# A low-rank gate as one contraction of 80 rows, and a rotary key whose weight parts share one tile

## The chip, the cores and the metric

The kernel runs on one core of a Trainium2 chip. The metric is the device time of one execution in microseconds (us). Before the change the median of three runs is 1384.74 us (1384.51 to 1385.14).

## The reference, cut to what matters

The model is a decoder trunk of two layers over 512 tokens of width 1024, in float32. Layer 0 mixes a Mamba-2 part (SSD) and gated linear attention (GLA), layer 1 is multi-head latent attention (MLA); each is followed by a SwiGLU FFN of hidden width 2816. Two small products matter here. In layer 0 the GLA forget gate comes from 16 columns of the input projection (`gk_low`) through a 16 x 512 matrix:

```python
gk = jax.nn.log_sigmoid((gk_low @ gk_w2 + gk_b).astype(jnp.float32)) / GLA_GATE_NORM
gcum = jnp.cumsum(gk.reshape(bsz, nc, Q, H, DK), axis=2)
...
q_dec = q * jnp.exp(gcum).astype(dtype)
k_inv = k * jnp.exp(-gcum).astype(dtype)
```

In layer 1 the last 32 columns of `h @ w_dqkv` are the rotary key that all 16 heads share:

```python
cq, ckv, k_rope = jnp.split(h @ w_dqkv, [MLA_Q_RANK, MLA_Q_RANK + MLA_KV_RANK], axis=-1)
...
k_rope = apply_rope(rms_norm(k_rope, k_rope_norm), cos, sin)
```

## The kernel before, in words

Activations lie transposed, features on the partitions and the 512 tokens along the free dimension, in eight tiles of 128 x 512. A dense product is computed on TensorE in the type fp32r: both factors are split into a rounded part and the remainder (`hi`, `lo`), and `mm3` (L140) issues three matmuls per tile of the contraction, hi by hi, hi by lo and lo by hi, all into one PSUM bank. `dense` (L145) runs `mm3` over the eight tiles of the contraction, so a block of 128 output features costs 24 matmuls of 512 columns.

`weight` (L124) brings the weights of a block: one DMA on SP's queue into a `wraw` tile (2 buffers), a cast on ScalarE into `whi` (L135, 3 buffers), a subtraction on VectorE into `wlo` (L136, 3 buffers).

The order on each engine is set by a planner when the program is built. It walks the program with timing estimates of its own and gives each engine, among the instructions whose operands and buffers are free, the one that stands earliest in the program. `weight` moves its three instructions 90 places forward in that order (`AHEAD`, L25). On the chip each engine then runs its list strictly in that order and waits on semaphores.

Three places matter for the change.

- L257 to L261: a 48-column projection gives 16 step sizes (rows 0 to 15) and `gk_low` (rows 32 to 47); VectorE scales it into `dg`. Four transposes (L269) read rows 0 to 15, and the step sizes go on from there, beside the convolutions (L313) of the SSD part, whose first products are the matmuls of L340.
- L470 to L489: behind the SSD part the pool `gla` opens in the memory that the SSD pool used. `w2`, the 16 x 512 gate matrix, is loaded on ScalarE's queue. For each of four heads one matmul in plain fp32 (L481: 16 rows, 128 x 512 out) writes the PSUM bank `st`, of which there is one; ScalarE takes the absolute value (L482), VectorE the minimum (L483). Then come one exponential (L484), one logarithm (L485), a subtraction (L486) and four scans (L488). `inner(0)` multiplies queries and keys by exponentials of the scan (L513, L529), and the matmuls of L548 to L550 read these. `out_round(1)`, half of the first two thirds of an output projection, is traced inside `inner(0)` and supplies other matmuls meanwhile.
- L689 to L693: at the start of MLA, behind FFN 0, a 32-column `dense` gives the rotary key (24 matmuls with 32 output rows), copied into `krr`. Five 128-column blocks of the same input follow (L700 to L702, `w_dqkv`), and then the transposes of `krr` (L739). The 32-column weights come through `weight`, so 90 places early.

A ring of two 128 x 512 tiles in the pool `res` with the tag `sq` holds squares for the norms: those of `Norm` (L196), `ysq` of the SSD part (L460) and `osq` of GLA (L586).

Of the kernel before, what the change touches and what calls it, by code (L numbers as in the profile page):

```python
# [8 lines left out]
F32 = mybir.dt.float32  # L9
F32R = mybir.dt.float32r  # L10
I32 = mybir.dt.int32
AF = mybir.ActivationFunctionType
ALU = mybir.AluOpType
# [4 lines left out]
P = 128  # L18
T = 512
D = 1024  # L20
KD = 8
# [24 lines left out]
def kernel(ctx: ExitStack, tc: tile.TileContext, A, yT, stop=99):  # L46
    nc = tc.nc
    V, S, G, E = nc.vector, nc.scalar, nc.gpsimd, nc.tensor

    const = ctx.enter_context(tc.tile_pool(name="const", bufs=1))  # L50
    res = ctx.enter_context(tc.tile_pool(name="res", bufs=1))
    wp = ctx.enter_context(tc.tile_pool(name="wp", bufs=3))
# [5 lines left out]
    def nm(s):  # L58
        cnt[0] += 1
        return f"{s}_{cnt[0]}"  # L60

    def acc():
        return pacc.tile([P, T], F32, tag="acc", name=nm("acc"))
# [11 lines left out]
    def aux(tag="st"):  # L75
        while isinstance(phase["tags"][tag], str):
            tag = phase["tags"][tag]
        return phase["p"].tile([P, T], F32, tag=tag, name=nm(tag), bufs=phase["tags"][tag])
# [13 lines left out]
    def col(name, i=0, lo=0, hi=P):  # L92
        j = PV[name] + i
        return pv[lo:hi, j:j + 1]
# [29 lines left out]
    def weight(src, kc, m):  # L124

        with tc.high_priority(offset=AHEAD):
            return weight_now(src, kc, m)

    def weight_now(src, kc, m):
        raw = wp.tile([P, KD * P], F32, tag="wraw", name=nm("wraw"), bufs=2)  # L130
        r = raw[:, :kc * m]
        nc.sync.dma_start(r.rearrange("p (k m) -> p k m", k=kc), src)
        hi = wp.tile([P, KD * P], F32R, tag="whi", name=nm("whi"))
        lo = wp.tile([P, KD * P], F32R, tag="wlo", name=nm("wlo"))
        S.copy(hi[:, :kc * m], r)  # L135
        V.tensor_tensor(lo[:, :kc * m], r, hi.bitcast(F32)[:, :kc * m], ALU.subtract)  # L136
        return (hi[:, :kc * m].rearrange("p (k m) -> p k m", k=kc),
                lo[:, :kc * m].rearrange("p (k m) -> p k m", k=kc))

    def mm3(out, ah, al, bh, bl, first, last):  # L140
        E.matmul(out, ah, bh, start=first, stop=False)  # L141
        E.matmul(out, ah, bl, start=False, stop=False)  # L142
        E.matmul(out, al, bh, start=False, stop=last)  # L143

    def dense(ps, w, xs):  # L145

        n = len(xs)
        for k, (xh, xl) in enumerate(xs):
            mm3(ps, w[0][:, k, :], w[1][:, k, :], xh, xl, k == 0, k == n - 1)
# [82 lines left out]
    R = nrm.done()  # L232
    xp = nrm.parts
# [20 lines left out]
    with tc.tile_pool(name="gkp", bufs=1) as gkp:  # L254
        rtok = tok_scalar(R)

        w = weight(A["w_dtgk"], KD, 48)  # L257
        ps = aux("a1")
        dense(ps[:48], w, xp)
        dg = gkp.tile([48, T], F32, name="dg")  # L260
        V.tensor_tensor(dg, ps[:48], R[:48], ALU.mult)  # L261
        dtb = gkp.tile([P, 16], F32, name="dtb")
        nc.scalar.dma_start(dtb, A["dt_bias"].partition_broadcast(P))
        alog = gkp.tile([P, 16], F32, name="alog")
# [2 lines left out]
        ps = aux()  # L267
# [26 lines left out]
        ps = aux()  # L294
# [6 lines left out]
        ps = aux()  # L301
# [6 lines left out]
        with tc.tile_pool(name="ssd", bufs=2) as sp:  # L308
            cw = sp.tile([P, 60], F32, name="cw", bufs=1)
            j = PV["conv_w"]  # L310
# [136 lines left out]
            for f in range(8):  # L447
# [12 lines left out]
                sq = res.tile([P, T], F32, tag="sq", name=nm("ysq"), bufs=2)  # L460
# [9 lines left out]
        with tc.tile_pool(name="gla", bufs=2) as gp:  # L470
            rmask = gp.tile([P, T], F32, name="rmask", bufs=1)
            G.memset(rmask, 1.0)
            G.memset(rmask.rearrange("p (c j) -> p c j", c=8)[:, :, 0:1], 0.0)
            w2 = gp.tile([48, T], F32, name="w2", bufs=1)
            nc.scalar.dma_start(w2[32:48, :], A["gk_w2"])

            ga = gp.tile([P, 4, T], F32, name="ga", bufs=1)
            gm = gp.tile([P, 4, T], F32, name="gm", bufs=1)
            for h in range(4):
                ps = aux()  # L480
                E.matmul(ps, w2[32:48, h * P:(h + 1) * P], dg[32:48, :], start=True, stop=True)  # L481
                S.activation(ga[:, h, :], ps, AF.Abs, bias=col("gk_b", h))  # L482
                V.tensor_scalar(gm[:, h, :], ps, col("gk_b", h), 0.0, ALU.add, ALU.min)  # L483
            S.activation(ga, ga, AF.Exp, scale=-1.0)  # L484
# [180 lines left out]
    R = mla_norm.done()  # L665
    xp = mla_norm.parts
    with tc.tile_pool(name="mla", bufs=2) as mp, tc.tile_pool(name="mla1", bufs=1) as m1:
# [18 lines left out]
                        pattern=[[-1, P]], channel_multiplier=1)  # L686


        w = weight(A["w_kr"], KD, 32)  # L689
        ps = acc()  # L690
        dense(ps[:32], w, xp)
        krr = m1.tile([32, T], F32, name="krr")
        V.tensor_copy(krr, ps[:32])  # L693


        lora, cf = {}, {}
        for who, n0, n in (("q", 0, 3), ("kv", 3, 2)):
            lora[who], ssq = [], None
            for c in range(n):
                w = weight(A["w_dqkv"][n0 + c], KD, P)  # L700
                ps = acc()
# [7 lines left out]
                sq = res.tile([P, T], F32, tag="sq", name=nm("lsq"), bufs=2)  # L709
# [4 lines left out]
            ps = aux()  # L714
# [22 lines left out]
        ps = aux()  # L737
# [14 lines left out]
        ps = aux()  # L752
# [247 lines left out]
```

## Time and profile before

| | |
|---|---|
| median of three runs | 1384.74 us |
| the profiled execution | 1385.21 us |
| its span on the core | 1383.5 us |
| TensorE (PE) busy | 1357.4 us, 98% of the span |
| VectorE (DVE) busy | 782.3 us, 57% |
| ScalarE (ACT) busy | 558.9 us, 40% |
| GpSimd (POOL) busy | 8.0 us, 1% |

The profile is of one execution. An engine is busy while it has an instruction in flight; matmuls are pipelined, so a matmul's own duration (0.39 us for 512 columns in fp32r) is longer than the distance from one start to the next. The chain of waits follows the work that ended last backwards and gives each piece of it the time by which it moved the end. "Idle before" in brackets is how long an engine stood before an instruction, and whose end it waited for. PEld is the weight load of TensorE, ACTq and SPq are the queues from which ScalarE and SyncE issue DMAs.

### The profile page before, as it was taken

Reading aid. Unit: us, or ns where it says so; the run is one execution under the profiler, and the core shown is the slowest. Engines: PE = TensorE matmul, PEld = TensorE weight load, DVE = VectorE, ACT = ScalarE, POOL = GpSimd, SP = SyncE. Lnnn points to the kernel's source line nnn. Section 1 sums busy time; section 2 is a strip of 40 time slices with the busy share of each in tenths; the row PEclk is TensorE's granted clock in tenths of the full one; section 3 lists DMA queues with packets and bytes.
Section 4 is the critical chain, followed back from the end, with each engine's and each line's share of the span. In section 5 each row is a group of like instructions: output and inputs, shape, how many; then the busy total and the mean of one; then the engine's idle time right before and its main releaser. Section 6 shows DMA issues by size and latency. Waiting matters only on the chain.

```text
span 1383.5 us, 16956 instructions
## 1 busy us (share of the span) xinstructions
PE 1357.4 (98%) x6650; PEld 1094.1 (79%) x6650; DVE 782.3 (57%) x1375; ACT 558.9 (40%) x934; POOL 8.0 (1%) x38
## 2 busy tenths in 40 slices
PE   7999999999999999999999999999999999999998
PEld 5798888677788888888888787667588888888887
DVE  7877966767757444444333449876684444443221
ACT  5675623543334323323223238775653233232221
POOL 0000000000000000000000000000000000000000
PEclk9999999999999999999999999999999999999999
DMA  5343132212233233233333321111032333333331
GB/s 175 108 143 102 61 106 78 63 61 76 62 105 93 91 93 106 92 98 100 92 90 107 90 66 59 52 46 62 1 92 91 103 95 92 101 97 107 104 108 64
DMA packets 36719, 122.19 MB, mean 88 GB/s; under 512 B 4736, under 2 KB 5760, under 8 KB 36640
## 3 DMA queue, kind: packets, MB, share of 16 engines
q1 hardware_dynamic: 35600, 120.70, 28.4%
q8 instruction: 53, 0.87, 0.3%
q10 hardware_dynamic: 1040, 0.41, 0.1%
q14 instruction: 26, 0.21, 0.0%
HBM read 118.96 MB, written 2.13 MB: 88 GB/s over the span
## 4 chain that ended last, share of the span: by engine, by line
PE 91%; DVE 6%; ACT 1%; issue 1%; DMA 1%; SPq 0%; ACTq 0%; DVEq 0%
PE acc L142 27%; PE acc L141 27%; PE acc L143 27%; PE sco L853 2%; PE ptr L867 1%; PE po L876 1%; DVE wlo L136 1%; PE st L175 1%; PE a L409 1%; PE a L579 1%; ACT whi L135 1%; PE a L395 0%; DMA x<-in_xT_dram 0%; PE a L581 0%; PE a L413 0%
## 5 line engine op out<-in xcount | busy, mean ns | idle before, releaser
L135 ACT CAST whi<-wraw 128x1024 fp32r<-128x1024 f32 (+2 forms) x223 | 226.7, 1018 | 570.9 <-PE acc L142 510.1
L141 PE MATMUL acc<-xh,whi 128*128 128x512 f32 (+1 forms) x1152 | 452.5, 393 | 2.8 <-ACT qT L836 1.6
L143 PE MATMUL acc<-xh,wlo 128*128 128x512 f32 (+1 forms) x1152 | 452.0, 393 | 0.0
L142 PE MATMUL acc<-xl,whi 128*128 128x512 f32 (+1 forms) x1152 | 451.7, 392 | 0.0
L136 DVE TENSOR_TENSOR wlo<-wraw,whi 128x1024 fp32r<-128x1024 f32 (+2 forms) x223 | 263.0, 1180 | 177.4 <-ACT whi L135 177.0
L141 PEld LDWEIGHTS acc<-xh,whi 128*128 128x128 f32 (+1 forms) x1152 | 215.7, 187 | 49.3 <-ACT qT L836 1.8
L142 PEld LDWEIGHTS acc<-xl,whi 128*128 128x128 f32 (+1 forms) x1152 | 215.8, 187 | 47.3 <-issue 3.3
L143 PEld LDWEIGHTS acc<-xh,wlo 128*128 128x128 f32 (+1 forms) x1152 | 215.8, 187 | 45.0 <-issue 0.9
L141 PE MATMUL acc<-fhh,whi 128*128 128x512 f32 x288 | 112.0, 389 | 0.0
L142 PE MATMUL acc<-fhl,whi 128*128 128x512 f32 x288 | 112.0, 389 | 0.0
L143 PE MATMUL acc<-fhh,wlo 128*128 128x512 f32 x288 | 112.0, 389 | 0.0
L637 DVE TENSOR_TENSOR fu<-acc,R 128x512 f32<-128x512 f32 x44 | 30.4, 691 | 139.4 <-PE acc L143 139.4
L634 DVE TENSOR_TENSOR fg<-acc,R 128x512 f32<-128x512 f32 x44 | 30.4, 692 | 94.0 <-PE acc L143 90.1
L143 PEld LDWEIGHTS acc<-fhh,wlo 128*128 128x128 f32 x288 | 54.1, 188 | 11.2
L141 PEld LDWEIGHTS acc<-fhh,whi 128*128 128x128 f32 x288 | 54.1, 188 | 11.2
L142 PEld LDWEIGHTS acc<-fhl,whi 128*128 128x128 f32 x288 | 54.1, 188 | 11.2
L141 PE MATMUL acc<-mxh,whi 128*128 128x512 f32 x128 | 49.7, 391 | 1.3 <-ACT whi L135 1.3
L142 PE MATMUL acc<-mxl,whi 128*128 128x512 f32 x128 | 49.9, 391 | 0.0
L143 PE MATMUL acc<-mxh,wlo 128*128 128x512 f32 x128 | 49.8, 390 | 0.0
L853 PE MATMUL sco<-kT,qT 96*128 96x128 f32 (+3 forms) x128 | 42.8, 445 | 1.5 <-DVE mx L856 1.3
L858 ACT ACTIVATE sc<-sc,mx 128x128 f32<-128x128 f32 (+3 forms) x64 | 35.7, 561 | 7.3 <-DVE mx L856 7.0
L856 DVE CUSTOM_DVE_ANT_0 sc<-sco,am 128x128 f32<-128x128 f32 (+3 forms) x64 | 30.7, 487 | 13.6 <-PE sco L853 11.5
(290 smaller groups left out, 1546.8 us busy)
## 6 DMA issues: line engine op xcount, KB each, us to landing
wraw<-in_w_gate_dram SPq DMA_DIRECT2D x44, 512.0 KB, 3.6
wraw<-in_w_up_dram SPq DMA_DIRECT2D x44, 512.0 KB, 3.6
wraw<-in_w_down_dram SPq DMA_DIRECT2D x32, 512.0 KB, 3.6
wraw<-in_w_out_dram SPq DMA_DIRECT2D x16, 512.0 KB, 3.6
wraw<-in_w_xbc_dram SPq DMA_DIRECT2D x12, 512.0 KB, 3.7
wraw<-in_w_down_dram SPq DMA_DIRECT2D x16, 384.0 KB, 3.1
wraw<-in_w_z_dram SPq DMA_DIRECT2D x8, 512.0 KB, 3.7
wraw<-in_w_v_dram SPq DMA_DIRECT2D x8, 512.0 KB, 3.6
```

Of the source, the lines that this page charges most:

```text
L135: S.copy(hi[:, :kc * m], r)
L136: V.tensor_tensor(lo[:, :kc * m], r, hi.bitcast(F32)[:, :kc * m], ALU.subtract)
L141: E.matmul(out, ah, bh, start=first, stop=False)
L142: E.matmul(out, ah, bl, start=False, stop=False)
L143: E.matmul(out, al, bh, start=False, stop=last)
L175: E.matmul(pb[:, c * P:(c + 1) * P], sel[:, c, :], y, start=True, stop=True)
L409: E.matmul(pd[64 * h:64 * h + 64, c * P:(c + 1) * P], xdt[:, c, h, :], mt[:, h, c, :], start=True, stop=True)
L634: V.tensor_tensor(g, pg, R, ALU.mult)
L637: V.tensor_tensor(u, pu, R, ALU.mult)
L853: E.matmul(ps[:, :n], qts[j][:, b * P:(b + 1) * P], kts[j][:, :n], start=True, stop=True)
L856: V.tensor_tensor_reduce(sc[:, :n], ps[:, :n], am[:, T - n:], -scale, 3e38, ALU.add, ALU.min, mx[:, j:j + 1])
L858: S.activation(sc[:, :n], sc[:, :n], AF.Exp, bias=mx[:, j:j + 1], scale=-1.0, accum_out=sm[:, j:j + 1])
```

## The change

The gate's factors are split too, but the three products are laid one below the other in one contraction. `gx` holds `gk_low` rounded in rows 0 to 15 and 32 to 47 and its remainder in rows 64 to 79; `gw` holds the remainder of the gate matrix in rows 0 to 15 and the rounded matrix in rows 32 to 47 and 64 to 79. The other rows are zero. One fp32r matmul of 80 rows per head replaces the fp32 matmul of 16 rows. `dg`, `w2` and the scratch tile `wt` come from the ring `sq`; `gx` and `gw` take the places of `dg` and `w2`.

For the rotary key the rounded weights lie twice and the remainder once side by side in one tile, 96 columns per tile of the contraction. Two matmuls per tile (with the high and the low part of the input) replace three; the remainder's product comes out in PSUM rows 64 to 95 and is added to rows 0 to 31. The weights no longer go through `weight`: their load, two casts and one subtraction stand at their own place in the program.

```diff
-        dg = gkp.tile([48, T], F32, name="dg")
-        V.tensor_tensor(dg, ps[:48], R[:48], ALU.mult)
+        dg = res.tile([P, T], F32, tag="sq", name="dg", bufs=2)
+        V.tensor_tensor(dg[:48], ps[:48], R[:48], ALU.mult)
+        gx = gkp.tile([80, T], F32R, name="gx")
+        G.memset(gx.bitcast(I32), 0)
+        S.copy(gx[32:48, :], dg[32:48, :])
+        S.copy(gx[0:16, :], dg[32:48, :])
+        V.tensor_tensor(gx[64:80, :], dg[32:48, :], gx[32:48, :].bitcast(F32), ALU.subtract)
...
-            w2 = gp.tile([48, T], F32, name="w2", bufs=1)
-            nc.scalar.dma_start(w2[32:48, :], A["gk_w2"])
+            gw = gp.tile([80, T], F32R, name="gw", bufs=1)
+            G.memset(gw.bitcast(I32), 0)
+            w2 = res.tile([P, T], F32, tag="sq", name="w2", bufs=2)
+            wt = res.tile([P, T], F32R, tag="sq", name="wt", bufs=2)
+            for j in (0, 32, 64):
+                nc.scalar.dma_start(w2[j:j + 16, :], A["gk_w2"])
+            S.copy(wt[0:16, :], w2[0:16, :])
+            V.tensor_tensor(gw[0:16, :], w2[0:16, :], wt[0:16, :].bitcast(F32), ALU.subtract)
+            for j in (32, 64):
+                S.copy(gw[j:j + 16, :], w2[j:j + 16, :])
...
-                E.matmul(ps, w2[32:48, h * P:(h + 1) * P], dg[32:48, :], start=True, stop=True)
+                E.matmul(ps, gw[:, h * P:(h + 1) * P], gx, start=True, stop=True)
...
-        w = weight(A["w_kr"], KD, 32)
+        wkr = wp.tile([P, KD * P], F32, tag="wraw", name="wkr", bufs=2)
+        wkr = wkr[:, :KD * 32].rearrange("p (k m) -> p k m", k=KD)
+        nc.sync.dma_start(wkr, A["w_kr"])
+        w3 = wp.tile([P, KD * P], F32R, tag="whi", name="w3")
+        w3 = w3[:, :KD * 96].rearrange("p (k j m) -> p k j m", k=KD, j=3)
+        for j in range(2):
+            S.copy(w3[:, :, j, :], wkr)
+        V.tensor_tensor(w3[:, :, 2, :], wkr, w3[:, :, 0, :].bitcast(F32), ALU.subtract)
         ps = acc()
-        dense(ps[:32], w, xp)
+        for k, (xh, xl) in enumerate(xp):
+            wk = w3[:, k].rearrange("p j m -> p (j m)")
+            E.matmul(ps[:96], wk, xh, start=(k == 0), stop=False)
+            E.matmul(ps[:96], wk, xl, start=False, stop=(k == KD - 1))
         krr = m1.tile([32, T], F32, name="krr")
-        V.tensor_copy(krr, ps[:32])
+        S.copy(krr, ps[64:96])
+        V.tensor_tensor(krr, ps[:32], krr, ALU.add)
```

## Rows read from the trace of the kernel before

**Rows 1.** The page: busy time, share of the span, instructions of each engine.
```profile
PE 1357.4 (98%) x6650; PEld 1094.1 (79%) x6650; DVE 782.3 (57%) x1375; ACT 558.9 (40%) x934; POOL 8.0 (1%) x38
```

**Rows 2.** Waits of PE over the span: us in total, times, longest.
```profile
PE a L548 <- DVE ki L529: 1.6, 1, 1.6
...
PE acc L141 <- ACT whi L135: 1.3, 1, 1.3
```

**Rows 3.** Chain of waits around the first gate matmul: start, us, what.
```profile
238.49 1.05 PE st L481 x2
239.53 0.43 PE acc L142
239.97 0.23 PE acc L143
```

**Rows 4.** Timeline: first matmul of the rotary key, first behind its last; start, us, what.
```profile
786.64 0.39 PE L141 MATMUL acc<-xh,whi 128*32 128x512 f32 x1
...
792.62 0.39 PE L141 MATMUL acc<-xh,whi 128*128 128x512 f32 x1
```

**Rows 5.** Timeline from the gate matrix's load to where PE stands waiting.
```profile
235.54 0.34 ACTq L475 DMA_DIRECT2D w<-in_gk_w_dram  x1
235.65 0.53 POOL L472 MEMSET rmask<- 128x512 f32 x1 [82.98 <-DVE mxl L121]
236.03 1.06 ACT L135 CAST whi<-wraw 128x1024 fp32r<-128x1024 f32 x1 [1.75 <-PE acc L142]
...
239.57 0.69 ACT L482 ACTIVATE ga<-st,pv 128x512 f32<-128x512 f32 x1 [2.49 <-PE st L481]
...
240.29 0.75 DVE L483 TENSOR_SCALAR gm<-st,pv 128x512 f32<-128x512 f32 x1 [1.95 <-ACT ga L482]
...
241.50 1.12 PE L481 MATMUL st<-dg,w 16*128 16x512 f32 x2
...
248.83 0.69 ACT L482 ACTIVATE ga<-st,pv 128x512 f32<-128x512 f32 x1 [2.40 <-PE st L481]
...
263.96 0.69 DVE L529 TENSOR_TENSOR ki<-kr,e 128x512 f32<-128x512 f32 x1
...
264.70 0.27 PE L548 MATMUL a<-qd,ki 128*64 128x64 f32 x1 [1.63 <-DVE ki L529]
...
266.33 0.47 PE L141 MATMUL acc<-mxh,whi 128*128 128x512 f32 x1 [1.29 <-ACT whi L135]
```

**Rows 6.** Timeline: last reader of a tile of the ring sq, ScalarE behind it.
```profile
223.29 0.69 DVE L463 TENSOR_TENSOR ysq<-ysq,ysq 128x512 f32<-128x512 f32 x1 [0.70 <-ACT ysq L461]
...
226.60 0.47 ACT L443 ACTIVATE v<-acc,rtok 128x256 f32<-128x256 f32 x1 [2.98 <-PE acc L143]
```

**Rows 7.** Timeline: subtractions that free a raw weight tile, around the rotary key.
```profile
787.70 1.22 DVE L136 TENSOR_TENSOR wlo<-wraw,whi 128x1024 fp32r<-128x1024 f32 x1 [0.17 <-ACT whi L135]
...
793.79 1.22 DVE L136 TENSOR_TENSOR wlo<-wraw,whi 128x1024 fp32r<-128x1024 f32 x1
```

**Rows 8.** DMA issues by line: count, KB each, median us to landing.
```profile
wraw<-in_w_kr_dram SPq DMA_DIRECT2D x1, 128.0 KB, 2.1
```

**Rows 9.** The tile krr: ns min/median/max, first and last start in us.
```profile
L739 PE MATMUL sco<-ident,krr x4: 221/222/243, 827.9 to 828.1; 32*128 32x32 f32 x4
```

**Rows 10.** Timeline around the scaled projection dg and the first SSD products.
```profile
29.93 0.68 DVE L261 TENSOR_TENSOR dg<-a,R 48x512 f32<-48x512 f32 x1 [0.68 <-ACT R L177]
...
39.22 0.68 DVE L330 SCALAR_TENSOR_TENSOR cT<-cvt,cva 128x512 f32<-128x512 f32 x1
...
39.95 0.19 PEld L340 LDWEIGHTS a<-cT,bT 128*128 128x128 f32 x1
```

**Rows 11.** A stretch at the start: us, busy us (count) by engine, PEclk, DMA share, GB/s.
```profile
6.00:12.20 6.20, 5.45 (x13) 2.06 (x14) 5.02 (x8) 6.12 (x11) 0.00 (x0) 1.00 1.04 389
```

**Rows 12.** Timeline: two neighbouring matmuls of that stretch.
```profile
11.33 0.63 PE L142 MATMUL a<-xl,whi 128*48 128x512 f32 x1
...
11.75 0.55 PE L143 MATMUL a<-xh,wlo 128*48 128x512 f32 x1
```

## The prediction

> **What bounds the kernel now.** I read the page's busy times first. TensorE (PE) has work in flight for 1357.4 of 1383.5 us [rows 1], so a microsecond taken from its queue is a microsecond off the end, unless PE stands waiting later for something that did not move. Hence the second view, the waits of PE over the whole span. It is short, and two of its entries lie just behind the gate: 1.6 us at L548 for a VectorE product and 1.3 us for a weight cast on ScalarE [rows 2]. The third view, the chain of waits, gives what one gate matmul and one ordinary fp32r matmul cost in PE's queue [rows 3], and the timeline gives what hangs on the gate [rows 5]. Around the rotary key PE runs without a gap, 24 matmuls and a norm's eight small ones in 792.62 - 786.64 = 5.98 us [rows 4]. So the two halves of the change sit in different places: the key's where PE alone is the limit, the gate's where a chain of ScalarE and VectorE work ends last.
>
> **The key's matmuls, removed from PE.** 24 become 16. An ordinary matmul moves the chain by 0.23 us [rows 3], and the 32-row form runs at the same pitch, since 24 x 0.23 = 5.5 us fits into the 5.98 of [rows 4] with the norm's eight. The trace has no 96-row form; between 32 and 128 output rows the pitch does not change, so I take 0.23. That is 8 x 0.23 = 1.84 us off PE. Its bounds are 0 and 1.84: no gain only if PE is short of something else there.
>
> **The key's other work.** The load, one cast more and one subtraction per set leave the early place that `weight` gave them; a cast or copy of this size is under the 0.73 to 1.22 us that any ScalarE or VectorE row of [rows 5, 7] shows. The copy out of PSUM becomes a ScalarE copy and a VectorE sum. Nobody needs `krr` soon: its first reader is PE's transposes at 827.9 us [rows 9], 35 us behind the last key matmul. The matmuls of five `w_dqkv` blocks, 24 x 0.23 = 5.5 us each, are the cover. I cost this at 0; the case without cover is rival D. On SP's queue the key's load now follows the first two, perhaps three, loads of `w_dqkv`, which `weight` still pulls 90 places forward, and these come earlier for it.
>
> **The gate's matmuls, removed from PE.** One costs 1.05 us and makes the next matmul cost 0.43 instead of 0.23 [rows 3]: 1.25 us. An fp32r matmul of 512 columns costs 0.23; the 80-row form is not in the trace, but fewer contraction rows than 128 can hardly cost more, and I see no reason for less. So PE's queue shrinks by 4 x (1.25 - 0.23) = 4.08 us. This is the upper bound of the gain, not the gain: PE then arrives 4.08 us sooner at L548, where it already waited 1.63 us for `ki`, and then 1.29 us for a cast [rows 5]. That cast is queued on ScalarE behind an exponential that itself waits for `ki`. What counts is how much sooner `ki` comes.
>
> **The gate's chain.** There is one bank `st`, so the four heads go round one after the other: matmul, absolute value on ScalarE, minimum on VectorE, next matmul. A round takes (248.83 - 239.57) / 3 = 3.09 us [rows 5]. In it the matmul itself holds 1.12 us; an fp32r one holds 0.39 [rows 4]. If nothing else in the round moves, each is 0.73 us shorter, and up to the fourth absolute value there are three rounds and one more matmul: 4 x 0.73 = 2.9 us. If PE's fixed order makes a round wait for ordinary matmuls, less; bounds 0 and 2.9.
>
> **When the first round can begin.** The gate matrix is now built in steps. Its raw load needs only a slot of the ring `sq`, whose last reader but one ends at 223.29 + 0.69 = 223.98 us, with ScalarE, whose queue issues it, idle for 2.98 us before 226.60 [rows 6]. Before, it was issued at 235.54, when the SSD pool had closed [rows 5]. So the three loads, the rounding and their arrival lie in idle time. `gw` itself still needs that pool: its zeroing on POOL comes behind the 0.53 us of `rmask` from 235.65, another 0.53, to 236.7 us; then ScalarE's cast to 237.09 [rows 5] and two copies of 512 columns at no more than 0.69 (the nearest ScalarE row) end at 238.5, with the remainder on VectorE beside them (0.68, as `dg` [rows 10]) or up to 0.7 later. Before, the first matmul ended at 239.57 at the latest and lasted 1.12, so it began by 238.45. The start moves by 0 to +0.7 us; I take +0.3. Loads that would still be issued at 235.54 give about +2.
>
> So `ki` comes 2.9 - 0.3 = 2.6 us sooner, and I take 2.6 us for the gate, between 0 (nothing of the round is won) and 4.08 (PE finds other work, and no wait grows). It could even exceed 4.08, by the 1.63 + 1.29 us of the old waits, if the planner deals the order anew.
>
> **The early part.** Behind `dg`, ScalarE gets two copies (at most 0.69 each) and VectorE one subtraction (0.68). VectorE feeds the first SSD products: `cT` ends at 39.90 us and its reader on PE loads at 39.95 [rows 10]. There is no slack, so what VectorE loses can pass to PE in full: bounds 0 and 0.7 + 0.4 = 1.1 us. I take 0.4, since the subtraction must first wait for the copy and can fall into VectorE's own waits. The zeroing on POOL (0.53, 8.0 us busy in all [rows 1]) is free.
>
> **Sum.** -1.84 - 2.6 + 0.4 = -4.0 us. The profiled execution took 1385.21 us, 1.71 around its span; that makes 1381.2 in it. It stood 0.47 above the median of 1384.74, against which the forecast is 1380.7 us.
>
> **Rivals.**
>
> A is the forecast: 1380.7, with a range of its own of 1379.3 to 1382.0.
>
> B, the gate's gain is waited away. If the rounds stay near 3.09 us because the planner spaces the gate's matmuls among ordinary ones as before, PE waits 4 us longer at L548 and only the key's part and the early cost are left: 1384.74 - 1.84 + 0.4 = 1383.3. For it speaks that PE's order is fixed by the planner's estimates; against it, that ScalarE stood idle for the matmul, 2.49 us before the first absolute value and 2.40 before the fourth [rows 5].
>
> C, PE's full saving arrives: -1.84 - 4.08 = -5.9, 1378.8. For it speaks that only 2.92 us of waiting stand in that place, and a different order of the cast and the exponential would remove 1.29 of them; against it, that L548 already waits.
>
> D, the other side: PE runs dry between FFN 0 and MLA. The key's load has lost its early place. It gets a raw tile when the subtraction at 787.70 ends, 788.92, or the one at 793.79, 795.01 [rows 7]; 2.1 us for the load [rows 8] and some 1.3 for casts and subtraction make 792.3 or 798.4. If PE's list has the key's matmuls first, as the program has them, PE waits from 786.64 [rows 4] for 5.7 or 11.8 us: with the other terms +1.7 or +7.8 us, 1386.4 to 1392.5, in the middle 1389. It decides as soon as that wait exceeds 4.0 us. Each `w_dqkv` block that stands ahead takes 5.5 us off it; those weights are there in time, and the planner takes what is ready, which speaks against it. Its clock for the load is an estimate, which speaks for it.
>
> [...]
>
> **How the numbers follow.** A 0.42, B 0.21, C 0.14, D 0.12, E 0.11. A measurement of this kernel tells 0.2%, 2.8 us, from no change, so faster means under 1381.97. Of A 0.38 falls there, and all of C; with a little from B and E that makes 0.54 faster. B, E, the rest of A and the mild end of D are within it: 0.31. D's heavy end, and a late gate matrix joined to a full early cost, give 0.15 slower. The range reaches down to 1377.0, C with some of the old waits gone, and up to 1387.0, D's light end; about 0.07 is left out below and 0.11 above.
>
> **What would show it.** Right: 4 gate matmuls of about 0.39 us, rounds near 2.4 us, the first absolute value near 239 us, `ki` some 2.6 us sooner than 263.96, and PE's wait at L548 longer by 1 to 1.5 us; 16 key matmuls with 96 rows at a pitch of 0.23, amid or behind the `w_dqkv` blocks, without idle time before them. Wrong: rounds of 3 us (B), no wait at L548 (C), a gap of several microseconds after 786 us (D), matmuls 0.42 us apart behind L548 (E), or a difference that arises in a stretch that neither half touches, from a new order of the whole list.

## The result, and the profile after

The changed kernel takes 1379.82 us (median of six executions, 1378.77 to 1381.92), the kernel before 1385.67 us beside it on the same chip (six executions, 1384.51 to 1391.07): ratio 0.9948, 95% interval 0.9934 to 0.9962. A second set on another chip gave 1378.51 us against 1386.36, ratio 0.9944 (0.9931 to 0.9958). One execution of the same kernel differs from the next by up to 6.6 us, in step with its mean granted clock (29 executions of the kernel before on one chip: 1384.67 to 1385.29 us at 1.000, 1388.59 to 1390.32 at 0.995 and 0.996); so stretches of two traces are compared here, and a stretch with a lower granted clock is named where there is one.

The page after, the busy row that answers to [rows 1]:

```profile
PE 1353.4 (98%) x6638; PEld 1095.5 (79%) x6638; DVE 784.1 (57%) x1377; ACT 562.3 (41%) x941; POOL 8.9 (1%) x40
```

PE has 12 instructions less (8 of the key's matmuls, and the four fp32 matmuls of the gate, each listed as two before). The profiled execution took 1379.86 us, 5.35 less than that of before. When the same VectorE and ScalarE instructions are matched in the two traces, the shift (after minus before) grows in three places:

| up to (us, before) | shift | gained or lost there |
|---|---|---|
| 235, ahead of the gate | -0.36 | -0.36 |
| 300, behind the gate | -5.63 | -5.27 |
| 780, end of FFN 0 | -5.59 | 0.04 |
| 820, behind the key | -7.00 | -1.41 |
| 890, attention | -5.72 | +1.3 |

The gate gave twice what I had put down, the key somewhat less, and 1.3 us were lost in a stretch that the change does not touch. The waits of PE between 230 and 300 us after, where [rows 2] had 1.6 at L548 (now L563) and 1.3 at L141:

```profile
PE acc L141 <- DVE x L243: 0.7, 1, 0.7
PE a L575 <- DVE sc L569: 0.7, 1, 0.7
PE st L496 <- ACT gw L490: 0.2, 1, 0.2
```

Both old waits are gone; nobody waits for `ki` any more. The gate's timeline after, against [rows 5]:

```profile
223.66 1.28 ACTq L486 DMA_DIRECT2D w<-in_gk_w_dram  x3
...
236.80 1.26 ACT L490 CAST gw<-w 16x512 fp32r<-16x512 f32 x2
...
238.11 0.50 PE L496 MATMUL st<-gx,gw 80*128 80x512 f32 x1 [0.20 <-ACT gw L490]
...
238.65 0.69 ACT L497 ACTIVATE ga<-st,pv 128x512 f32<-128x512 f32 x1 [0.59 <-PE st L496]
...
245.67 0.69 ACT L497 ACTIVATE ga<-st,pv 128x512 f32<-128x512 f32 x1 [1.93 <-PE st L496]
...
260.38 0.68 DVE L544 TENSOR_TENSOR ki<-kr,e 128x512 f32<-128x512 f32 x1
...
262.65 0.50 PE L141 MATMUL acc<-mxh,whi 128*128 128x512 f32 x1 [0.67 <-DVE x L243]
...
265.59 0.27 PE L563 MATMUL a<-qd,ki 128*64 128x64 f32 x1
```

The three loads run 12 us earlier than the old one. A round takes (245.67 - 238.65) / 3 = 2.34 us instead of 3.09. `ki` comes 3.58 us sooner. And the first product of `ki`, which held PE up before, now stands behind the whole output round, 4.5 us after `ki` is there.

What held PE up is seen in VectorE's order. The same stretch before:

```profile
249.50 0.69 DVE L243 TENSOR_TENSOR x<-x,acc 128x512 f32<-128x512 f32 x1 [2.28 <-PE acc L143]
...
252.23 0.69 DVE L243 TENSOR_TENSOR x<-x,acc 128x512 f32<-128x512 f32 x1 [1.38 <-PE acc L143]
254.95 0.69 DVE L243 TENSOR_TENSOR x<-x,acc 128x512 f32<-128x512 f32 x1 [2.03 <-PE acc L143]
255.56 2.29 DVE L486 TENSOR_TENSOR gm<-gm,ga 128x2048 f32<-128x2048 f32 x1
257.76 1.22 DVE L136 TENSOR_TENSOR wlo<-wraw,whi 128x1024 fp32r<-128x1024 f32 x1
258.89 4.57 DVE L488 TENSOR_TENSOR_SCAN gm<-rmask,gm 128x512 f32<-128x512 f32 x4
...
265.50 1.88 DVE L243 TENSOR_TENSOR x<-x,acc 128x512 f32<-128x512 f32 x3
```

and after:

```profile
245.30 0.69 DVE L243 TENSOR_TENSOR x<-x,acc 128x512 f32<-128x512 f32 x1 [0.22 <-PE acc L143]
...
248.42 0.69 DVE L243 TENSOR_TENSOR x<-x,acc 128x512 f32<-128x512 f32 x1 [1.27 <-PE acc L143]
...
251.14 0.69 DVE L243 TENSOR_TENSOR x<-x,acc 128x512 f32<-128x512 f32 x1 [0.64 <-PE acc L143]
252.51 2.29 DVE L501 TENSOR_TENSOR gm<-gm,ga 128x2048 f32<-128x2048 f32 x1 [0.68 <-ACT ga L500]
254.72 0.68 DVE L243 TENSOR_TENSOR x<-x,acc 128x512 f32<-128x512 f32 x1
255.31 4.56 DVE L503 TENSOR_TENSOR_SCAN gm<-rmask,gm 128x512 f32<-128x512 f32 x4
...
261.92 1.28 DVE L243 TENSOR_TENSOR x<-x,acc 128x512 f32<-128x512 f32 x2
```

The output round that fills PE here is a quarter of the output projection, 4 of its 16 contraction tiles (and not half of its first two thirds, as the description of the kernel has it). It has eight sums of 12 matmuls each (4 tiles x 3), and the sums take turns in a ring of three PSUM banks. A bank comes free when VectorE has added it to `x` (L243). Additions that are not done before the scan wait for the scan, `qd`, `ki`, `qp` and `e`: some 7 us in which no bank comes free. Before, three additions stood ahead of the scan, after four. PE can then issue as many sums as additions plus three banks: before 6 x 12 = 72 matmuls, 24 left at the stop; after 7 x 12 = 84, 12 left. The traces have just these numbers of the round's matmuls ahead of the stop. The first addition behind the scan ends at 265.50 + 0.69 = 266.19 us before, and PE goes on at 266.33 [rows 5]; after, at 261.92 + 0.68 = 262.60, and PE at 262.65.

So the entry "<- ACT whi L135" of [rows 2] is not the reason. The matmul at 266.33 opens the seventh sum, whose weights are the last of the round's four `w_out` loads. The raw weights have two tiles, so the next load but one, `w_k` of the second head, takes the tile of these weights; it is issued at 259.00 us, when their subtraction at 257.76 has ended (258.98). Their cast is therefore the one of 254.60, long done; the cast that the entry names ends at 266.24 and makes the weights loaded at 259.00, which this sum does not read:

```profile
254.60 1.03 ACT L135 CAST whi<-wraw 128x1024 fp32r<-128x1024 f32 x1
...
259.00 0.33 SPq L132 DMA_DIRECT2D wraw<-in_w_k_dram  x1
...
265.21 1.03 ACT L135 CAST whi<-wraw 128x1024 fp32r<-128x1024 f32 x1
```

The key after: its own first matmul and the first behind its last, against [rows 4], and then ScalarE and PE in the next block.

```profile
781.06 0.39 PE L716 MATMUL acc<-xh,w 128*96 128x512 f32 x1
...
785.21 0.50 PE L141 MATMUL acc<-xh,whi 128*128 128x512 f32 x1
...
791.88 0.69 ACT L733 ACTIVATE lh<-acc,pv 128x512 fp32r<-128x512 f32 x1
792.46 0.58 ACT L177 COPY R<-sco 128x512 f32<-128x512 f32 x1
...
792.60 0.40 PE L142 MATMUL acc<-xl,whi 128*128 128x512 f32 x1
793.09 0.66 PE L212 MATMUL sco<-ident,R 128*128 128x128 f32 x4
```

5.98 us became 4.15: 1.83 gained. But the first `w_dqkv` block now ends before the norm's `R` is copied out of PSUM; ScalarE takes that block's cast (`lh`) first, and `R` is copied 0.40 us behind the end of the matmuls that make it (792.06; they are L175), where it was 0.04 before. So the transposes at L212 stand 0.49 us behind their neighbour instead of 0.23 (798.09 and 798.32 before), and the next matmul another 0.06 later: 0.32 in all. Another 0.1 is lost just behind the interval of 4.15 us, because the norm's eight small matmuls now stand at its end: the matmul behind them, at 785.21, moves the next by 0.34 instead of 0.23. The load of the key's weights was issued at 764.4 us and cast from 771.55: long ahead of 781.06.

### The profile page after: what moved, and what is told of

The parts are those of the page before. It is cut to its first block, busy times and chain, and to the rows that moved or that the text cites. A ratio compares the mean times of both kernels' runs of the same rounds, so it can differ in the third digit from the quotient of the medians.

```text
span 1378.1 us, 16954 instructions
## 1 busy us (share of the span) xinstructions
PE 1353.4 (98%) x6638; PEld 1095.5 (79%) x6638; DVE 784.1 (57%) x1377; ACT 562.3 (41%) x941; POOL 8.9 (1%) x40
## 4 chain that ended last, share of the span: by engine, by line
PE 76%; DVE 5%; ACT 2%; issue 1%; POOL 0%; POOLq 0%; ACTq 0%
PE acc L142 23%; PE acc L141 23%; PE acc L143 23%; PE sco L880 2%; PE ptr L894 1%; PE po L903 1%; DVE wlo L136 1%; PE a L594 1%; PE st L175 0%; PE a L596 0%; DVE gm L503 0%; DVE sc L883 0%; ACT whi L135 0%; DVE kT L857 0%; DVE st L829 0%
## 5 line engine op out<-in xcount | busy, mean ns | idle before, releaser
L135 ACT CAST whi<-wraw 128x1024 fp32r<-128x1024 f32 (+2 forms) x222 | 226.2, 1019 | 564.7 <-PE acc L142 483.3
L141 PE MATMUL acc<-xh,whi 128*128 128x512 f32 x1144 | 449.6, 393 | 2.8 <-ACT qT L863 1.6
L142 PE MATMUL acc<-xl,whi 128*128 128x512 f32 x1144 | 449.0, 392 | 0.0
L143 PE MATMUL acc<-xh,wlo 128*128 128x512 f32 x1144 | 448.8, 392 | 0.0
L141 PEld LDWEIGHTS acc<-xh,whi 128*128 128x128 f32 x1144 | 214.9, 188 | 48.3 <-ACT qT L863 1.8
L142 PEld LDWEIGHTS acc<-xl,whi 128*128 128x128 f32 x1144 | 214.9, 188 | 45.8 <-issue 2.5
L143 PEld LDWEIGHTS acc<-xh,wlo 128*128 128x128 f32 x1144 | 215.0, 188 | 43.6 <-issue 0.5
L141 PE MATMUL acc<-fhh,whi 128*128 128x512 f32 x288 | 112.1, 389 | 0.0
L141 PEld LDWEIGHTS acc<-fhh,whi 128*128 128x128 f32 x288 | 54.1, 188 | 11.2
L141 PE MATMUL acc<-mxh,whi 128*128 128x512 f32 x128 | 49.8, 391 | 0.7 <-DVE x L243 0.7
```

## The experiments

Theory 1: the gate's gain is PE's saved queue time together with the old waits, because one more addition stands ahead of the scan and PE runs one sum further; the key's is 1.84 less what the copy of `R` takes back. Its rivals stand with each run. The numbers in brackets are 95% intervals; "shift" is against the profiled kernel before, in the stretch named.

**1. The gate alone.** The edit: the key's section of the kernel before put back.

> The gate as in the changed kernel, the rotary key as before. Theory 1 (the halves are independent, and the gate gives PE's saved queue time of 4.08 us plus most of the old waits behind it): 5.2 us faster than before, 0.3 us of it ahead of the gate, and the key's stretch as before. Rival (the gate is worth only its chain, as forecast, and the rest of the difference needs the key's change): 2.2 to 2.6 us faster.

1380.96 us against 1386.43, 0.9952 [0.9939, 0.9965]. The shift is -0.34 ahead of the gate and -5.72 behind it, 5.38 gained; the key's stretch stays at -5.70. Theory 1 holds, the rival falls: the gate's gain doesn't need the key.

**2. The key alone.** The edit: the gate and `dg` of the kernel before put back.

> The key as in the changed kernel, the gate as before. Theory 1: 1.4 us faster, as the trace of the changed kernel shows behind that stretch, with 8 x 0.23 = 1.84 us gained up to the first w_dqkv matmul and 0.4 us given back where PE waits at L212 for the copy of R, which then stands behind the cast of the first lora part on ScalarE. Rival (PE's saving arrives whole): 1.84 us faster.

1386.1 us against 1386.43, 0.9992 [0.9982, 1.0002]. In the key's stretch the shift goes from 3.1 to 1.7: 1.4 gained, as expected. But ahead of it this execution had lost 2.9 us where nothing is changed. After the two old waits (1.62 and 1.29 us here) PE runs at half pace:

```profile
264.95 0.27 PE L548 MATMUL a<-qd,ki 128*64 128x64 f32 x1 [1.62 <-DVE ki L529]
...
266.58 0.76 PE L141 MATMUL acc<-mxh,whi 128*128 128x512 f32 x1 [1.29 <-ACT whi L135]
267.14 0.63 PE L142 MATMUL acc<-mxl,whi 128*128 128x512 f32 x1
267.57 0.63 PE L143 MATMUL acc<-mxh,wlo 128*128 128x512 f32 x1
```

The stretch behind the wait has these rows (us, PE, PEld, DVE, ACT, POOL busy, granted clock, DMA share, GB/s), here and in the kernel before:

```profile
267.00:270.00 3.00, 3.00 (x8) 2.32 (x8) 2.70 (x5) 0.96 (x3) 0.00 (x0) 0.50 0.03 5
```

```profile
267.00:270.00 3.00, 3.00 (x15) 2.49 (x14) 3.00 (x6) 0.94 (x2) 0.00 (x0) 1.00 0.03 5
```

The granted clock is 0.50; thirteen matmuls stand 0.43 us apart instead of 0.23. Matmuls 0.42 us apart behind L548 are the sign that the prediction names for E. Here they come in a kernel with the old waits, and not in every execution: the same waits in the profiled kernel before, 1.63 and 1.29 us, were followed by 1.00. So the length of the wait alone does not decide it here.

**3. The score products behind the output round.** An edge in the kernel before (shown without the lines that hand `tail` through and the edge's arguments); in the trace the order of all other instructions is that of before, on every engine:

```diff
+                    if tail is not None and r == 0:   # tail: last matmul of out_round(1)
+                        for m in (m0, m1_):           # the first two score products
+                            tc.add_manual_dep(m.ins, tail.ins.name, ...)
```

> The kernel before with one edge more: the first two score products of head 0 come behind the last 24 matmuls of the output round, where the changed kernel has them. Nothing else moves on any engine. Theory 1 (PE ran out of PSUM banks: the matmul behind the products needs a bank that VectorE's addition frees at 266.19 us, and the additions stand behind the scan): no gain, 0 us plus or minus 0.3; PE stands some 3.2 us at L141 instead of 1.63 at L548 and 1.29 at L141. Rival (PE waited for ki): the 1.63 us go.

1387.81 us against 1386.43, 1.0003 [0.9993, 1.0013]. No gain: PE stands in one place (3.25 us) for as long as before in two, and then runs at half pace (matmuls 0.43 us apart, granted clock 0.60 from 265 to 268 us), so that the stretch loses 1.7 us, about as much as the half pace costs (some 1.6 us, experiment 8).

```profile
PE acc L141 <- ACT whi L135: 3.3, 1, 3.3
```

So nothing was lost by waiting for `ki`: with the products out of the way PE stands all the same. That the next matmul has no bank is what experiments 4 and 8 show.

**4. Two idle banks for the last two sums.** In the kernel before:

```diff
-                ps = acc()
+                ps = aux("a2") if r == 1 and m2 == 3 else acc()
```

> The kernel before with the last two of the eight sums of the output round in the two banks a2, which stand idle then, instead of the three of acc; PE then has the products behind them. Theory 1 (PSUM banks): both waits go, 2.5 to 3.2 us faster behind the gate. Rival (PE waited for the weight cast on ScalarE, as the page names it): PE still starts at 266.3 us, no gain; rival (PE waited for ki): 1.6 us.

1384.37 us against 1386.43, 0.9983 [0.9972, 0.9993]. Through the round PE's order is that of experiment 3, and only the banks differ. Both old waits are gone, and from 264 to 270 us PE is never idle:

```profile
264.00:270.00 6.00, 6.00 (x46) 4.85 (x45) 6.00 (x11) 3.04 (x5) 0.00 (x0) 1.00 0.05 16
```

That settles banks against the cast and against `ki`. But the shift goes only from -0.49 to -1.83 us, 1.3 gained and not 2.5 to 3.2. PE now comes early to the transposes behind the products, whose bank VectorE frees late:

```profile
272.52 0.52 PE L560 MATMUL a<-ident,kp 128*128 128x128 f32 x3 [1.39 <-DVE sc L554]
```

**5. The gate's matmuls five times.** In the kernel of experiment 1:

```diff
-                E.matmul(ps, gw[:, h * P:(h + 1) * P], gx, start=True, stop=True)
+                for _ in range(5):
+                    E.matmul(ps, gw[:, h * P:(h + 1) * P], gx, start=True, stop=True)
```

> The gate as in the changed kernel, the rotary key as before, but each of the four gate matmuls is issued five times into the same place (the same sum again): 5 x 0.23 = 1.15 us of PE's queue, near the 1.25 of before, with the early loads, the casts and gx kept. Theory 1 (the saved queue time of PE and the shorter round made the gain): 0 to 1.2 us faster than before, waits of 1.5 to 3 us behind the gate again. Rival (the early loads and the new deal of the order made it): 4 us or more faster.

1389.74 us against 1387.12, 1.0018 [1.0007, 1.0028]: slower, where I had expected 0 to 1.2 us faster. The rival falls by far: early loads and casts gain nothing here without the short matmul. Rounds are back at (248.70 - 239.68) / 3 = 3.01 us, and the planner's order is a worse one: two additions ahead of the scan, hence (2 + 3) x 12 = 60 matmuls and 36 left at the stop. So the run shows what the lost sums cost together with PE's queue time, and not the queue time by itself. The waits, longer than expected, and the clock behind them:

```profile
PE a L564 <- DVE ki L545: 3.5, 1, 3.5
PE acc L141 <- DVE x L243: 1.1, 1, 1.1
```

```profile
264.00:270.00 6.00, 4.95 (x15) 3.79 (x14) 4.49 (x8) 1.93 (x4) 0.00 (x0) 0.50 0.12 18
```

Here the profile names the addition itself.

**6. The gate's sums in two banks.** In the kernel before, fp32 as it was:

```diff
-                ps = aux()
+                ps = aux("a2")
                 E.matmul(ps, w2[32:48, h * P:(h + 1) * P], dg[32:48, :], start=True, stop=True)
```

> The kernel before with the gate's four sums in the two banks a2 in place of the single bank st: PE's work is unchanged, but the heads no longer go round one after the other, so the fourth absolute value comes some 4 us sooner, and with it the scan, ki and the additions. Theory 1: it can give back at most the old waits, 1.63 + 1.29 + 0.2: 2 to 3 us faster behind the gate, the 4.08 us of PE's queue stay. Rival (the chain alone made the changed kernel's gain of 5.3): 5 us faster. Rival (another wait takes its place, as behind e4): 1 to 1.5 us.

1388.87 us against 1387.12, 1.0007 [0.9995, 1.0020]. All three expectations missed. The fourth absolute value does come 5.67 us sooner, `ki` 2.9, but one addition only stands ahead of the scan: (1 + 3) x 12 = 48 matmuls, 48 left. The waits are 2.4 and 1.3 us. And the clock falls twice: behind the second wait (matmuls 0.43 us apart from 263.96 to 266.09 us, granted clock 0.81 from 264 to 270 us), and before that where PE had no idle time, at two pairs of fp32 matmuls:

```profile
237.80 1.98 PE L481 MATMUL a<-dg,w 16*128 16x512 f32 x4
...
240.83 2.29 PE L481 MATMUL a<-dg,w 16*128 16x512 f32 x4
...
243.65 0.63 PE L141 MATMUL acc<-xh,whi 128*128 128x512 f32 x1
```

```profile
240.00:246.00 6.00, 6.00 (x15) 3.41 (x15) 2.68 (x4) 3.79 (x4) 0.00 (x0) 0.70 0.16 61
```

So a chain that brings `ki` 2.9 us sooner gained nothing in an order with two additions fewer ahead of the scan. How much a shorter chain would gain in the order of before, this run doesn't show.

**7. Three edits on the changed kernel.** The banks of experiment 4, the transposes in `a2`, and an edge that puts the copy of `R` ahead of the first lora cast (`lh` of the first `w_dqkv` block).

> The changed kernel with three edits: the last two sums of the output round in the banks a2, the transposes behind the score products in a2 too, and the copy of R ahead of the first lora cast on ScalarE. Theory 1: the waits of 0.67 and 0.65 us at 262 to 269 us and the 0.4 us at L212 go: 1.2 to 1.7 us faster than the changed kernel in its stretches. Rival (VectorE is the bound there and the next wait takes their place): 0.4 us, from the key's stretch alone.

1380.14 us against 1387.12, 0.9944 [0.9927, 0.9961]: no better than the changed kernel's 0.9948 and 0.9944. In its trace the gate's stretch gains 0.4 to 0.5 us more than in the changed kernel's two traces and the key's 0.33 more (1.75 in all, nearly the whole 1.84). These 0.7 to 0.8 us lie between theory 1 (1.2 to 1.7) and the rival (0.4): a new wait of 1.1 us (PE L583 for ScalarE's copy of `kt`) took the place of the two old ones, as the rival has it for the gate, and the edge for `R` gave what theory 1 has for the key.

**8. One addition ahead of the scan.** In the kernel of experiment 3:

```diff
-                V.tensor_tensor(X[m], X[m], ps, ALU.add)
+                with tc.high_priority(offset=400 if r == 1 and m == 3 else 0):
+                    V.tensor_tensor(X[m], X[m], ps, ALU.add)
```

> The kernel of e3 (the kernel before with the first two score products behind the output round) and in it one addition of the round, that of the fourth sum, ahead of the scan on VectorE, where the changed kernel has it; a subtraction for weights moves behind the scan for it. Theory 1 (PE stands because its PSUM banks are freed by additions that stand behind the scan): PE waits for the subtraction only, to 264.8 us instead of 266.3 on the time axis of before, and then for nothing: the round ends 1.5 to 1.8 us sooner than in e3. Rival (PE's wait goes back to ki, which comes later now, or to the weight cast): no gain or 0.5 us slower.

1384.3 us against 1386.36, 0.9982 [0.9972, 0.9992]; experiment 3 had 1.0003. The wait of 3.25 us becomes one of 1.17, for the subtraction that the edit moved:

```profile
264.45 0.50 PE L143 MATMUL acc<-mxh,wlo 128*128 128x512 f32 x1 [1.17 <-DVE wlo L136]
```

The round ends at 269.66 us instead of 272.36. This execution had started 0.93 us later and experiment 3 lost some 1.6 us at half pace (eight pitches of 0.37 to 0.43 in place of 0.23), so 2.70 + 0.93 - 1.6 = 2.0 us are the order's, against 1.5 to 1.8 expected; 1.2 of them are given back by 280 us, where PE waits for what VectorE and ScalarE make of the products. It is the cleanest test of the bank rule: PE's order through the round is that of experiment 3, and on VectorE one addition of 0.69 us stands ahead of the scan and one subtraction of 1.22 us behind it. (Behind the round the planner's order differs from experiment 3, so the time of the whole execution proves less than this stretch.)

**9. Additions preferred in the changed kernel**, with the edge for `R`.

```diff
+                with tc.high_priority(offset=400 if r == 1 else 0):
+                    V.tensor_tensor(X[m], X[m], ps, ALU.add)
```

> The changed kernel with the additions of the output round preferred in VectorE's order (one then falls between two scans, one directly behind ki), and the copy of R ahead of the first lora cast on ScalarE; PE's order is unchanged. Theory 1: the wait of 0.67 us at 262.65 us goes, and 0.3 us at L212, 1.0 us in all; with fewer waits no slow matmuls behind the gate. Rival (what the additions win is lost by ki, which comes 0.6 us later, and by the score products behind it): 0.3 us, from L212 alone.

1378.68 us against 1386.36, 0.9945 [0.9932, 0.9957]; the changed kernel beside it 0.9944. The wait at L141 goes, and two others come (0.6 us for `kr` at L566, 0.8 at L576 for `sc`); the gate's stretch gains nothing, the key's 0.3. The rival is right: behind the scan PE's waits are for VectorE again, whichever of its instructions goes first.

**10. The changed kernel again.**

> The changed kernel once more, on the same chip as e9. Both theories: the order and the waits as before; whether the matmuls behind the wait for qT at 878 us run at half pace differs from one execution to the next, and with it 1.3 us of the time.

1378.51 us. From 280 to 870 us its instructions keep within 0.04 us of those of the first profile, and then the 1.3 us come back. The two profiles behind the same wait, first the first one, then this one:

```profile
879.58 0.59 PE L141 MATMUL acc<-whi,lh 128*128 128x384 f32 x1 [1.35 <-ACT qT L863]
879.97 0.52 PE L142 MATMUL acc<-wlo,lh 128*128 128x384 f32 x1
...
882.21 0.52 PE L143 MATMUL acc<-whi,ll 128*128 128x384 f32 x1
```

```profile
879.58 0.45 PE L141 MATMUL acc<-whi,lh 128*128 128x384 f32 x1 [1.35 <-ACT qT L863]
879.86 0.34 PE L142 MATMUL acc<-wlo,lh 128*128 128x384 f32 x1
...
881.08 0.34 PE L143 MATMUL acc<-whi,ll 128*128 128x384 f32 x1
```

The wait is the same to a hundredth; from 879.00 to 882.50 us the granted clock is 0.60 in the first and 1.00 in the second. The change doesn't cause it: of the profiled executions, those of experiments 1, 3, 4, 6 and 8 (all but the first with the gate of before) lose 1.2 to 2.4 us in the same stretch against the kernel before, and those of experiments 2, 5, 7 and 9 lose nothing there.

## Why the prediction came out near, and which steps failed

**The time.** 1380.7 forecast, 1379.82 measured. The time is near in part by luck. The difference that was forecast, -4.0 us, is not near: the changed kernel is 5.85 us below the kernel beside it, and 7.85 on the second chip. The forecast was taken from the median of three executions, 1384.74, and the kernel before has a higher one in each later set (1385.67 to 1387.12). In the profiles two errors cancel: the gate gave 2.7 us more than forecast, and 1.3 us of half pace at 880 us (granted clock 0.60), which no term of the sum had, went the other way. Without that half pace the profiled execution would have taken some 1378.6 us, 6.6 below the profile before.

**The gate's term was mis-sized: -2.6 forecast, -5.3 measured.** The round's size was right (4 x 0.73 less, 3.09 to 2.34) and so was the start (the first absolute value 0.92 us sooner, some 0.3 of it the execution's own start; forecast 0.73 - 0.3 = 0.43). `ki` came 3.58 us sooner: 2.25 from three rounds, 0.92 from the start and 0.42 on the way from the fourth absolute value to `ki`, since an addition of 0.68 us stands between L501 and the scan in place of a subtraction of 1.22. What failed is the step "What counts is how much sooner `ki` comes". It took the two waits at their names. PE stood for a PSUM bank, and what counts is how soon VectorE's first addition behind the scan ends (3.59 sooner) and how many sums stand ahead of it: one more, 12 x 0.227 = 2.7 us. Of these 6.3 us some 0.3 are the execution's own start; 1.1 are given back by 280 us, 0.65 of it in the new wait at L575 (the rest I have not traced), and 0.35 come again by 300, 0.22 of them the old wait at L560. Put the other way, by PE's queue as rival C had it: PE's 4.08 us, and the old waits of 2.92 and 0.22, less 0.67, 0.65 and 0.20 of new ones, make 5.7; 5.3 are measured, and 0.24 of the rest is that the four 80-row matmuls move PE's queue by 0.23 to 0.34 us each, 1.16 in all, and not by 4 x 0.23. The text had allowed this ("if the planner deals the order anew"), as an exception beyond its own upper bound of 4.08; it was the case.

**B** would have kept rounds of 3 us; they are 2.34. **C**'s mechanism is what happened at the gate, with the old waits on top, and its sign came: no wait at L548. **E**, matmuls 0.42 us apart behind L548, did come in some runs, but the change shortens the waits behind which they came: a granted clock of 0.50 behind the old waits of 1.62 and 1.29 us (experiment 2) and of 0.60 behind the one of 3.25 (3), of 0.50 and 0.81 behind longer ones (3.5 and 1.1 us in 5, 2.4 and 1.3 in 6), but no such stretch there in the five profiles with the short gate matmul issued once (the changed kernel's two and experiments 1, 7 and 9; granted clock 1.00 from 230 to 300 us in the changed kernel's first, and a mean over the whole execution of 0.999 in experiment 1 and 1.000 in the other three). No run shows what makes the clock fall, so E's 0.11 was an estimate of mine. The 1.00 that [rows 11] lists at the start of the kernel is not a measured clock: the trace's first entry for the clock stands at 12.1 us, and from 12.14 on the pitch is 0.23. The 0.42 us of [rows 12] is the pitch that experiment 2 shows at 0.50 (0.42 to 0.43). Of the 67 executions of the kernel before beside the experiments, 30 have a mean clock of 0.998 or less, and 1 of 11 of the changed one. That part of the gain I had not put down at all; it isn't separated from the rest, since the clock of each execution isn't known by stretch.

**D** was wrong at its root: the key's load did not fall behind the `w_dqkv` loads, as the part on the key's other work has it. It stayed ahead of all five, as before: issued at 764.37 us where it was 769.96, earlier by the 5.59 of the whole stretch, and 17 us ahead of its matmuls. So it waited for neither subtraction of [rows 7], which free the tiles of `w_dqkv` blocks, and had no part in the time.

**The key: -1.84 forecast, -1.41 measured, and -1.4 in experiment 2.** Matmuls and pitch were right (1.83). "I cost this at 0" failed for a neighbour: PE, being earlier, reached the transposes of `R` before ScalarE had copied it. That is 0.32 us, and experiments 7 and 9 gave 0.3 back; the last 0.1 is the pitch behind the norm's small matmuls.

**The early part: +0.4 forecast.** From 25 to 30 us up to 110 to 140 us the shift changes by -0.02 to +0.30, median 0.17, in six traces with `gx`, and by -0.33 to +0.11, median -0.04, in five without. So some +0.2, hardly above the scatter. The -0.36 of the table comes from the start of the execution, which differs by -0.82 to +0.31 between kernels that are the same there.

**Open.** Why the clock falls behind a wait in one execution and not in the next, and which stretches have the lower clock in four of experiment 7's six timed executions, whose mean clock is 0.997. Nor do the runs price PE's queue time and the one more sum apart: experiments 5 and 6, which were to do so, changed the order of the additions too.

## What to carry to other kernels

Where PE waits and the profile names a producer, look up which tile the waiting matmul really reads and whose bank it writes: count the sums that fit into the ring (readers done so far plus banks) and see whether PE stopped just there. If it did, the gain of a shorter chain is counted in whole sums, by the number of readers that get ahead of the long instruction on the engine that frees the banks (here one addition more ahead of the scan, one sum of 12 matmuls, 2.7 us). And a stretch that the change does not touch may still move by more than the change (experiment 2: 2.9 us lost ahead of the key, 1.4 gained at it): match the instructions of two executions of the same kernel before explaining it.

## What was not expected of the hardware

Two pairs of plain fp32 matmuls with 16 contraction rows (1.98 and 2.29 us, ordinary matmuls between them) were followed by matmuls 0.43 us apart and a granted clock of 0.70 and 0.73 over 12 us, with no idle time on PE (experiment 6); the four single ones of the kernel before, one in each round of 3.09 us, were not (granted clock 1.00 from 235 to 252 us). The forms that the trace of before lacked keep the pitch in a row: 0.23 us with 96 output rows, and with 80 contraction rows five in a row take 1.33 us (experiment 5), four pitches of 0.235 and a last matmul of 0.39. A single one of 80 rows moved the next by 0.23 to 0.34 in the changed kernel.
